# The down projection's left operands, made by the up projection's steps

## The chip, the cores and the metric

The kernel runs on one core of one Trainium2 chip. The number that counts is the device time of one execution in microseconds (us), as the median of several runs. The five engines are called as in the profile: PE (TensorE, the matmuls; PEld is its weight load), DVE (VectorE), ACT (ScalarE), POOL (GpSimd) and SP (SyncE, which here issues nearly all DMAs, in order).

## The reference: what is computed

One decoder block for 2048 tokens of width 1024, in float32. A norm and a combined input projection feed two token mixers that run side by side (a state space model with a GLU, and a delta-rule recurrence), whose outputs go through one output projection and are added to the input. The change touches only what comes after that, the MLP and the last norm:

```python
hn = rms_norm(h, norm_ffn_g[i])
h = h + jnp.square(jax.nn.relu(hn @ w_up[i].astype(F32))) @ w_down[i].astype(F32)
return rms_norm(h, norm_final_g).astype(x.dtype)
```

`w_up` is 1024 x 4096 and `w_down` 4096 x 1024, so the hidden layer is 2048 tokens x 4096.

## The kernel before

**Float32 out of three matmuls.** Every operand x is split into two numbers with few significant bits: hi is ACT's cast of x (L374, or L1418 in the up projection), lo is x - hi, computed on DVE (L377, L1419). A product of two operands is hi*hi + hi*lo + lo*hi, three matmuls per 128 rows of the inner dimension, all accumulated in one PSUM bank (`product`, L1328).

**Seven products instead of eight.** Both MLP projections use Winograd's form of Strassen's scheme once. Each operand is cut into four quarters a, b, c, d; seven products of sums of quarters give the four quarters of the result. `left_sums` makes the seven left operands, in the order 1, 5, 6, 2, 7, 3, 4 (`ORDER`): a; c + d; (c + d) - a; b; a - c; b - ((c + d) - a); d. Three of them (1, 2 and 4) are plain quarters and four (5, 6, 7 and 3) are sums, one tensor operation each (L1291, L1294, L1297, L1300). `right_sums` does the like for the right operand, again four operations (L1309, L1311, L1315, L1318). One PSUM bank A takes products 1, 6, 7 and 4 after each other and is read after each; bank X takes 5 and then 3; bank B takes 2.

**Up projection (`mlp_up`).** Its left operand is `w_up`, its right operand the normed rows of h. There are two halves of 1024 tokens (`hb`) and in each 16 steps (`f`) of 256 hidden columns, so 32 steps of seven products of twelve 512-wide matmuls. For each step 1 MB of weights is loaded (L1408) into the ring of eight buffers called `raw`, the left sums are made on POOL, and the halves go to a ring of 16 tiles, `ys`, from which PE loads them; they are made two products ahead (`UA`, class `Ahead`). What comes out of the seven products are four tiles of 128 hidden columns by 512 tokens: ACT copies a bank to SBUF (L1469), DVE adds another bank to it (L1495, L1498, L1501), and `finish` squares the relu: ACT relu (L1463), POOL square (L1464), then a store of 256 KB to DRAM, `hid_d` (L1465), on SP's queue. In the very last step three of the four tiles have relu and square in one DVE operation (L1461) and all four stores are on POOL's queue. When the first half of the tokens ends, the right operands of the second half are made (`xs`, L1397 and L1398, their sums on POOL).

**Down projection (`mlp_down`).** Its left operand is the hidden layer, its right operand `w_down`. Eight groups of 512 hidden rows each take all eight chunks of 256 tokens; a chunk of a group is seven products of six 512-wide matmuls. The 16 sums tiles `acc` (1024 wide, h at first) stay in SBUF. In a group's first chunk the seven right operands are taken; they are made from 2 MB of raw weights by DVE and ACT, in nine slots `w0` to `w8`, two products ahead (`DW`). The left operands are made anew for every chunk and group: two loads of 256 KB from `hid_d` (L1538, four buffers `hraw`), four sums 256 wide on POOL, seven casts on ACT and seven low halves on DVE, three products ahead (`DH`). Of a chunk's seven additions to `acc`, three go over an ACT copy (L1564) and POOL (L1560, from tile `c`), and four are DVE's, straight from PSUM (L1560). In the last group each chunk's rows are normed (ACT square into `junk`, L1594; DVE, L1596) and stored.

**Order.** The kernel is written in a framework that schedules the instructions of each engine by priority (the order of the program) against a model of time, gives tiles their buffers, and sets the waits. Each engine and each DMA queue then works in order. The first right and left operands of the down projection have high priority.

Of the kernel before, what the change touches and what calls it, by code (L numbers as in the profile page):

```python
# [15 lines left out]
P = 128  # L16
# [14 lines left out]
def exp_exact(nc, pool, out, x, n, tag):  # L31
    """out = exp(x), rounded to about one unit in the last place; 0 below the normal range."""
# [26 lines left out]
def sincos(nc, pool, s_out, c_out, x, n, tag):  # L59
# [42 lines left out]
    # even quadrant keeps (s, c), odd swaps them  # L102
# [11 lines left out]
def s5_params(K, lam_re, lam_im, log_dt, b_re, b_im, c_re, c_im, d_skip):  # L114
    """Everything of the state space that depends on the parameters alone.
    Rows of the 128 partitions: (re | im half, state 64); G = 32 groups of H = 16 channels; chunks of 16 tokens."""
# [4 lines left out]
    with pool_of(tc, name="s5p", bufs=1) as sp:  # L121
# [21 lines left out]
        # powers 0 .. 16 of exp(lam dt)  # L143
# [17 lines left out]
        # f = (exp(lam dt) - 1) / lam  # L161
# [17 lines left out]
        # b_bar, both halves  # L179
# [13 lines left out]
        # c, states on partitions, both halves  # L193
# [10 lines left out]
        # coefficient rows: c * power -> (re, -im), b * power -> (re, im)  # L204
# [13 lines left out]
        # chunk step exp(lam dt 16): [128 = (group half, state), re/im, 16 groups]  # L218
# [8 lines left out]
        # powers 1 .. 16 of the chunk step: real part, and -/+ imaginary part  # L227
# [21 lines left out]
def s5_core(K, u_dram, g_dram):  # L249
    """u_dram, g_dram: [2048, 512] token rows; g = gelu(state space of u + d_skip u)."""  # L250
# [17 lines left out]
    def out_rows(g):  # L268
        """two groups' c * power, [128, 2, 17 powers x 16 channels]"""
# [7 lines left out]
    for g in range(0, G, 2):  # L277
# [4 lines left out]
        # two groups' channels, newest token of a chunk first  # L282
# [30 lines left out]
    # running state over the 128 chunks, rows (group half, state), re and im side by side: within 8 segments of 16 chunks ...  # L313
# [11 lines left out]
    # ... then from segment to segment  # L325
# [55 lines left out]
def rms_rows(K, pool, ss, n, width, tag):  # L381
    """(ss / width + eps) ** -0.5 of [128, n] sums of squares."""
# [7 lines left out]
def norm_transposed(K, pool, ps_tile, rows, gain, dest, done=None):  # L390
    """rows: 4 tiles [128 tokens, 1024]; dest(k): where hi, lo go of rows * rms * gain, features 128 k .. on partitions."""
# [19 lines left out]
def norm_transposed_1(K, pool, ps_tile, row, gain, dest):  # L411
    """the same of one tile of 128 tokens, into dest[k]"""
# [16 lines left out]
def mm3(K, out, pairs):  # L429
    """out = sum over pairs of (lhs hi + lo)^T (rhs hi + lo) without the lo lo products (below float32's last bit)."""  # L430
# [1251 lines left out]
```

## Time and profile before

| | |
|---|---|
| median of three runs | 2687.09 us (2685.21 to 2688.03) |
| profiled execution, first to last instruction | 2688.6 us, taken as its own time |
| up projection, first to last matmul | 1272.6 to 1931.6 us |
| down projection, first matmul to the add of its last sum | 1938.3 to 2680.0 us |
| busy over the whole span | PE 92%, DVE 71%, POOL 52%, ACT 47% |
| mean granted TensorE clock | 0.968 |

A row of the table of stretches has the length and then the busy time of each engine with its number of instructions, the granted clock, the busy share of the DMA engines and the GB/s. A row of a group has line, engine, operation, output and inputs, shape, count, then busy time in us and mean ns of one, then the idle time just before them and what ended it. Rows of the chain of waits and of the timeline begin with the start and the length in us.

### The profile page before, as it was taken

How to read it: one execution, taken by the hardware profiler on the slowest of the kernel's cores; microseconds unless marked ns; L12 is line 12 of the kernel's file. 1: busy time of each engine (PE TensorE's matmuls, PEld its weight loads, DVE VectorE, ACT ScalarE, POOL GpSimd, SP SyncE). 2: the span in 40 equal slices, each digit the busy share in tenths (PEclk: the TensorE clock that was granted, in tenths of full speed). 3: DMA queues.
4: the chain of work that ended last, by engine and by line, in shares of the span. 5: the costliest groups of instructions: out<-in, count | busy, mean ns of one | idle time of the engine just before them, and what ended most of it. 6: DMA issues, size and time to landing. Idle time of an engine off the chain costs nothing. (4 is left out here: it accounts for less than half of the span.)

```text
span 2688.6 us, 38819 instructions
## 1 busy us (share of the span) xinstructions
PE 2476.8 (92%) x13084; PEld 2030.6 (76%) x13084; DVE 1906.8 (71%) x3212; ACT 1276.2 (47%) x2683; POOL 1387.2 (52%) x1261
## 2 busy tenths in 40 slices
PE   7999989998998989999999998999888899899987
PEld 7887667786888878887788877888666667677765
DVE  7468796679777868666844577444478878887877
ACT  6355545554444455454544444444334444444444
POOL 1068787503222233121655577555466666677666
PEclk9999989998989999999999999999899999999999
DMA  9555748896867453444453325232532212221213
GB/s 296 191 172 171 215 121 259 246 240 169 174 156 158 112 181 133 156 138 156 149 171 108 110 79 170 96 110 79 199 116 77 75 54 76 75 76 52 77 63 125
DMA packets 451799, 375.11 MB, mean 140 GB/s; under 512 B 182192, under 2 KB 382896, under 8 KB 451600
## 3 DMA queue, kind: packets, MB, share of 16 engines
q1 hardware_dynamic: 450992, 370.54, 46.1%
q8 instruction: 103, 1.69, 0.3%
q10 hardware_dynamic: 288, 1.05, 0.1%
q0 software_dynamic: 320, 1.05, 0.1%
q14 instruction: 96, 0.79, 0.1%
HBM read 245.55 MB, written 121.77 MB: 137 GB/s over the span
## 5 line engine op out<-in xcount | busy, mean ns | idle before, releaser
L1560 POOL TENSOR_TENSOR acc<-acc,c 128x512 f32<-128x512 f32 x192 | 282.2, 1488 | 43.2 <-ACT c L1564 42.9
L1464 POOL TENSOR_TENSOR c<-c 128x512 f32<-128x512 f32 x125 | 159.6, 1277 | 147.4 <-ACT c L1463 138.6
L377 DVE TENSOR_TENSOR hl<-hraw,hh 128x256 fp32r<-128x256 f32 x256 | 196.3, 785 | 28.8 <-ACT hh L374 28.2
L433 PE MATMUL ps_z<-xh,wh 128*128 128x512 f32 x448 | 184.6, 412 | 16.6 <-DVE zr L617 7.0
L1419 DVE TENSOR_TENSOR wl<-wraw,wh 128x512 fp32r<-128x512 f32 x128 | 154.1, 1217 | 52.6 <-ACT wh L1418 52.6
L374 ACT CAST hh<-hraw 128x256 fp32r<-128x256 f32 x256 | 103.3, 407 | 165.9 <-PE ps_da L1328 102.9
L435 PE MATMUL ps_z<-xh,wl 128*128 128x512 f32 x448 | 181.9, 406 | 0.0
L434 PE MATMUL ps_z<-xl,wh 128*128 128x512 f32 x448 | 181.3, 405 | 0.0
L374 ACT CAST hh<-hs 128x256 fp32r<-128x256 f32 x192 | 77.6, 406 | 190.3 <-PE ps_da L1328 90.3
L1419 DVE TENSOR_TENSOR wl<-ws,wh 128x512 fp32r<-128x512 f32 x96 | 92.4, 966 | 97.1 <-PE ps_ua L1328 57.5
L1560 DVE TENSOR_TENSOR acc<-acc,ps_dx 128x512 f32<-128x512 f32 x128 | 87.0, 680 | 95.4 <-POOL acc L1560 95.0
L1291 POOL TENSOR_TENSOR hs<-hraw 128x256 f32<-128x256 f32 x64 | 51.9, 810 | 167.8 <-DMA hraw<-hid_d 97.4
L913 POOL TENSOR_TENSOR DT<-dtc,cst 128x128 f32<-128x128 f32 x128 | 56.1, 469 | 158.9 <-PE ps_pq L920 106.1
L1418 ACT CAST wh<-ws 128x512 fp32r<-128x512 f32 x96 | 59.5, 620 | 145.3 <-PE ps_ua L1328 92.7
L377 DVE TENSOR_TENSOR hl<-hs,hh 128x256 fp32r<-128x256 f32 x192 | 122.8, 641 | 1.4 <-ACT hh L374 1.4
L433 PEld LDWEIGHTS ps_z<-xh,wh 128*128 128x128 f32 x448 | 87.6, 196 | 41.3 <-DVE zr L617 8.8
L1418 ACT CAST wh<-wraw 128x512 fp32r<-128x512 f32 x128 | 79.1, 619 | 80.7 <-PE ps_ua L1328 39.3
L1564 ACT COPY c<-ps_da 128x512 f32<-128x512 f32 x192 | 105.6, 583 | 14.4 <-PE ps_da L1328 14.4
L609 DVE TENSOR_TENSOR wl<-wr,wh 128x1024 fp32r<-128x1024 f32 x56 | 86.3, 1541 | 34.9 <-ACT wh L608 33.7
L433 PE MATMUL ps_o<-woh,ys 128*128 128x512 f32 x256 | 102.5, 401 | 1.5 <-ACT ys L1114 1.0
L435 PEld LDWEIGHTS ps_z<-xh,wl 128*128 128x128 f32 x448 | 87.3, 195 | 19.3 <-issue 0.5
L434 PEld LDWEIGHTS ps_z<-xl,wh 128*128 128x128 f32 x448 | 87.5, 195 | 18.7 <-issue 1.1
(673 smaller groups left out, 8434.5 us busy)
## 6 DMA issues: line engine op xcount, KB each, us to landing
wraw<-in_w_up SPq DMA_DIRECT2D x64, 512.0 KB
hraw<-hid_d SPq DMA_DIRECT2D x128, 256.0 KB
hid_d<-c SPq DMA_DIRECT2D x124, 256.0 KB
wr<-in_w_in SPq DMA_DIRECT2D x56, 512.0 KB
xrow<-in_x SPq DMA_DIRECT2D x32, 512.0 KB
wraw<-in_w_down SPq DMA_DIRECT2D x16, 1024.0 KB
aq<-f_d SPq DMA_DIRECT2D x32, 256.0 KB
ba<-f_d SPq DMA_DIRECT2D x64, 128.0 KB
```

The costliest lines, as they stand in the source:

```text
L374: nc.scalar.copy(out=hi, in_=raw)
L377: (lo_eng or nc.vector).tensor_tensor(out=lo, in0=raw, in1=hi.bitcast(F32), op=ALU.subtract)
L433: K.nc.tensor.matmul(out, lh, rh, start=i == 0, stop=False)
L434: K.nc.tensor.matmul(out, lh, rl, start=False, stop=False)
L435: K.nc.tensor.matmul(out, ll, rh, start=False, stop=i == n - 1)
L609: v.tensor_tensor(out=wl, in0=wr, in1=wh.bitcast(F32), op=ALU.subtract)
L913: g.tensor_tensor(out=DT[:, p], in0=bc(dtc[:, u, p:p + 1, :], [P, 4, 32]), in1=c["m4"].rearrange("p (a x) -> p a x", a=4), op=ALU.mult)
L1418: act.copy(out=hi, in_=o)
L1419: v.tensor_tensor(out=lo, in0=o, in1=hi.bitcast(F32), op=ALU.subtract)
L1464: g.tensor_tensor(out=o, in0=o, in1=o, op=ALU.mult)
L1560: add = lambda eng, o, s: eng.tensor_tensor(out=o, in0=o, in1=s, op=ALU.add)
L1564: act.copy(out=t, in_=ps)
```

## The change

The tiles that leave a step of the up projection are already the quarters that the down projection's `left_sums` needs, if its quarters are cut suitably: two neighbouring tiles of 128 hidden columns, and two blocks of 512 tokens. So the step itself makes the four sums (on DVE), their high halves (ACT) and low halves (DVE), and stores these eight tiles in `hs_d`; the three plain quarters are stored as they are, in `hr_d`. That makes eleven stores of 256 KB where there were four, all on SP's queue. The square goes from POOL to ACT, in every step; the last step has no special case any more, and product 4 is read by the relu without a copy before it.

The down projection loads, for two chunks at a time, the four ready operands (512 KB each, five buffers) and the three plain quarters (256 KB each, three buffers), and splits only the plain ones, 512 wide. Its rows of w and its token rows are paired anew to fit (`a i p`, `rows`). Of the three additions that POOL made, one (c2) goes to DVE. Tile counts change to make room: `raw` 8 to 7, `c` 5 to 3, and the last norm's `junk` shares the buffers of the loaded operands. The `ys` ring of 16 now also takes the hidden layer's halves.

```diff
-        raw = lambda shape, name: rp.tile(shape, F32, tag="raw", bufs=8, name=name)
+        raw = lambda shape, name: rp.tile(shape, F32, tag="raw", bufs=7, name=name)
...
+        def hid(name):
+            nonlocal ct
+            ct = (ct + 1) % 6
+            return hp.tile([P, BT], F32, tag="o", bufs=3, name=name) if ct < 3 else oc[0].tile([P, BT], F32, tag=("g2h", "g2l", "g2s")[ct - 3], name=name)
+
+        def operands(hb, fp, q, done):
+
+            def plain(n):
+                nc.sync.dma_start(out=hr_dram[hb, fp, PLAIN.index(n)], in_=q[n])
+
+            def split_(n, o):
+                hi, lo = (oy.tile([P, BT], F32R, tag="ys", bufs=16, name="h" + s) for s in "hl")
+                act.copy(out=hi, in_=o)
+                v.tensor_tensor(out=lo, in0=o, in1=hi.bitcast(F32), op=ALU.subtract)
+                for i, t in enumerate((hi, lo)):
+                    nc.sync.dma_start(out=hs_dram[hb, SPLIT.index(n), fp, i], in_=t.bitcast(F32))
+
+            if done in (1, 4):
+                plain(done)
+            elif done == 3:
+                a, c, d = q[1], q[3], q[4]
+                s = hp.tile([P, BT], F32, tag="s", bufs=2, name="hs")
+                v.tensor_tensor(out=s, in0=c, in1=d, op=ALU.add)
+                split_(5, s)
+                v.tensor_tensor(out=c, in0=a, in1=c, op=ALU.subtract)
+                split_(7, c)
+                q["s2"] = s2 = hp.tile([P, BT], F32, tag="s", bufs=2, name="hs2")
+                v.tensor_tensor(out=s2, in0=s, in1=a, op=ALU.subtract)
+                split_(6, s2)
+            else:
+                plain(2)
+                s = hp.tile([P, BT], F32, tag="s", bufs=2, name="hs3")
+                v.tensor_tensor(out=s, in0=q[2], in1=q["s2"], op=ALU.subtract)
+                split_(3, s)
...
-                def finish(o, fi, tb):
-                    if f == 30 and hb and (fi, tb) != (1, 0):
-                        v.scalar_tensor_tensor(out=o, in0=o, scalar=0.0, in1=o, op0=ALU.max, op1=ALU.mult)
-                    else:
-                        act.activation(out=o, in_=o, func=AF.Relu)
-                        g.tensor_tensor(out=o, in0=o, in1=o, op=ALU.mult)
-                    (nc.gpsimd if f == 30 and hb else nc.sync).dma_start(out=hid_dram[f + fi, :, (hb * 2 + tb) * BT:(hb * 2 + tb + 1) * BT], in_=o)
+                q = {}
+
+                def finish(o, name, src=None):
+                    act.activation(out=o, in_=o if src is None else src, func=AF.Relu)
+                    act.activation(out=o, in_=o, func=AF.Square)
+                    q[name] = o
+                    operands(hb, f // 2, q, name)
...
-                        c4 = t("c4")
-                        act.copy(out=c4, in_=A)
-                        finish(c4, 1, 0)
+                        finish(hid("c4"), 2, A)
...
         def hs():
...
+            for gr in range(NG):
+                for c in range(0, NC, 2):
+                    hb, tk, fs, ops = c // 4, slice(c % 4 * P, c % 4 * P + 256), slice(2 * gr, 2 * gr + 2), {}
+                    for i in range(2):
+                        for n in ORDER:
+                            if i:
+                                pass
+                            elif n in SPLIT:
+                                t = hp.tile([P, 2, 2, 256], F32R, tag="hs", bufs=5, name="hs")
+                                nc.sync.dma_start(out=t.bitcast(F32), in_=hs_dram[hb, SPLIT.index(n), fs, :, :, tk].rearrange("a l p t -> p a l t"))
+                                ops[n] = t[:, :, 0], t[:, :, 1]
+                            else:
+                                t = hp.tile([P, 2, 256], F32, tag="hr", bufs=3, name="hr")
+                                nc.sync.dma_start(out=t, in_=hr_dram[hb, fs, PLAIN.index(n), :, tk].rearrange("a p t -> p a t"))
+                                ops[n] = split(K, hp, t, [P, 2, 256], "h", 4)
+                            yield tuple([t[:, k, i * P:i * P + P] for k in range(2)] for t in ops[n])
...
-                    t = hp.tile([P, 512], F32, tag="c", bufs=5, name=name)
+                    t = hp.tile([P, 512], F32, tag="c", bufs=3, name=name)
                     act.copy(out=t, in_=ps)
-                    add(g, o, t)
+                    add(eng, o, t)
...
-                        later(a12, A, "c2")
+                        later(v, a12, A, "c2")
...
-                        junk = wp2.tile([P, 1024], F32, tag="junk", name="junk")
+                        junk = hp.tile([P, 1024], F32, tag="hs", bufs=5, name="junk")
```

The full diff also takes out comments all over the file, which changes line numbers little and no instruction.

More of the change, by code (lines that the diff above doesn't have):

```diff
@@ L1521, in mlp_down @@
         wpool, apool = [wp1] * 6 + [wp2] + [wp3] * 2, [rp] * 2 + [ap1] * 8 + [ap2] * 2 + [wp3] * 4
+        rows = lambda c: [(c // 4) * 1024 + i * BT + c % 4 * P for i in range(2)]
         def ws():
@@ L1533, in hs @@
         def hs():
-            for k in range(0, 32, 4):
-                for c in range(NC):
-                    r = [rp.tile([P, 2, 256], F32, tag="hraw", bufs=4, name="hraw") for _ in range(2)]
-                    for j in range(2):
-                        nc.sync.dma_start(out=r[j], in_=hid_dram[k + 2 * j:k + 2 * j + 2, :, c * 256:c * 256 + 256].rearrange("a p t -> p a t"))
-                    for o in left_sums(g, [[r[j][:, :, i * P:i * P + P] for j in range(2)] for i in range(2)],
-                                       lambda: hp.tile([P, 2, P], F32, tag="s", bufs=5, name="hs")):
-                        yield halves_of(K, hp, o, [P, 2, P], "h", 10)
+            for gr in range(NG):
[14 more added lines that the diff above has]
+                            yield tuple([t[:, k, i * P:i * P + P] for k in range(2)] for t in ops[n])
         w, hid = Ahead(ws(), DW), Ahead(hs(), DH)
-        acc, fin, first = [], None, None
+        acc, fin, first = {}, None, None
         with tc.high_priority():
@@ L1552, in mlp_down, with later @@
                   with tc.issue_after(first.ins) if c else ExitStack():
-                    for t in range(2 * c, 2 * c + 2):
-                        a = apool[t].tile([P, 1024], F32, tag=f"acc{t}", name=f"acc{t}")
-                        ld = nc.sync.dma_start(out=a, in_=h_dram[t * P:t * P + P, :])
-                        acc.append(a)
+                    for i in range(2):
+                        t = 2 * c + i
+                        acc[c, i] = apool[t].tile([P, 1024], F32, tag=f"acc{t}", name=f"acc{t}")
+                        ld = nc.sync.dma_start(out=acc[c, i], in_=h_dram[rows(c)[i]:rows(c)[i] + P, :])
                   first = first or ld
-                r0, r1 = acc[2 * c:2 * c + 2]
+                r0, r1 = acc[c, 0], acc[c, 1]
                 a11, a12, a21, a22 = r0[:, 0:512], r0[:, 512:], r1[:, 0:512], r1[:, 512:]
                 add = lambda eng, o, s: eng.tensor_tensor(out=o, in0=o, in1=s, op=ALU.add)
-                def later(o, ps, name):
-                    t = hp.tile([P, 512], F32, tag="c", bufs=5, name=name)
+                def later(eng, o, ps, name):
+                    t = hp.tile([P, 512], F32, tag="c", bufs=3, name=name)
                     act.copy(out=t, in_=ps)
-                    add(g, o, t)
+                    add(eng, o, t)
                 A, X, B = (psp.tile([P, BT], F32, tag=n, bufs=b, name="ps_d" + n) for n, b in (("a", 3), ("x", 2), ("b", 2)))
@@ L1596, in mlp_down @@
                         v.scalar_tensor_tensor(out=r, in0=r, scalar=rs, in1=fin, op0=ALU.mult, op1=ALU.mult)
-                        t0 = (2 * c + i) * P
-                        nc.sync.dma_start(out=out[0, t0:t0 + P, :], in_=r)
+                        nc.sync.dma_start(out=out[0, rows(c)[i]:rows(c)[i] + P, :], in_=r)
 _INS = ["x", "norm_mix_g", "w_in", "lam_re", "lam_im", "log_dt", "b_re", "b_im", "c_re", "c_im", "d_skip", "w_glu", "b_glu",
@@ L1627, in hybrid_block @@
         y_d = D([NT, 512], "y_d")
[L1628 removed]
+        x2_d, hs_d, hr_d = D([4, P, KT, BT], "x2_d"), D([2, 4, 16, 2, P, BT], "hs_d"), D([2, 16, 3, P, BT], "hr_d")
         A = lambda *names: [a[n] for n in names]
@@ L1661, in hybrid_block @@
             opened = out_proj(K, keep, a["x"], g_d, y_d, f_d, s_d, *A("g2", "ln_x_w", "ln_x_b", "w_glu", "b_glu", "s5_out_g", "w_out", "norm_ffn_g"), h_d, x2_d)
-            mlp_up(K, opened, h_d, x2_d, a["norm_ffn_g"], a["w_up"], hid_d)
-        mlp_down(K, h_d, hid_d, a["w_down"], a["norm_final_g"], out)
+            mlp_up(K, opened, h_d, x2_d, a["norm_ffn_g"], a["w_up"], hs_d, hr_d)
+        mlp_down(K, h_d, hs_d, hr_d, a["w_down"], a["norm_final_g"], out)
 def kernel(**inputs):
```

31 lines of the change are left out of this document (15 added, 16 removed).

## The prediction

> **What bounds the kernel now.** I read the busy shares first, then stretches of time: the up projection from its first matmul to its last, its undisturbed part, the down projection from its first matmul to the add of its last sum, and what is left behind it.
>
> ```profile
> PE 2476.8 (92%) x13084; PEld 2030.6 (76%) x13084; DVE 1906.8 (71%) x3212; ACT 1276.2 (47%) x2683; POOL 1387.2 (52%) x1261
> core 0: us, PE busy (x) PEld busy (x) DVE busy (x) ACT busy (x) POOL busy (x), PEclk, DMA share, GB/s
> 1272.60:1931.60 659.00, 636.66 (x2721) 510.95 (x2719) 360.14 (x357) 298.10 (x520) 382.34 (x268) 0.98 0.36 119
> 1660.00:1900.00 240.00, 240.00 (x1037) 193.79 (x1036) 113.36 (x123) 105.38 (x188) 129.26 (x99) 1.00 0.29 97
> 1938.30:2680.00 741.70, 662.88 (x2688) 509.18 (x2688) 605.07 (x819) 332.18 (x721) 512.37 (x460) 0.97 0.25 83
> 2680.00:2688.60 8.60, 0.00 (x0) 0.00 (x0) 3.38 (x5) 1.15 (x2) 1.10 (x2) 0.67 0.46 183
> ```
>
> PE is full in the undisturbed up projection (240 of 240 us); in the down projection DVE is at 605 of 742 us. Both stages issue 2688 matmuls. Their pace when nothing disturbs them is in the chain of waits, where the same product of two successive chunks begins 9.76 us apart:
>
> ```profile
> 2378.16 2.78 PE ps_da L1328 x12
> 2387.91 2.79 PE ps_da L1328 x12
> ```
>
> So a chunk (42 matmuls) costs 9.76 us, an up step (84) 19.52, and the 64 chunks 624.6 us. The down projection loses 741.7 - 624.6 = 117 us; the up projection 659.0 - 624.6 = 34, which its first steps and the change of token half lose. Cut into chunks, the sixth group of the down projection reads (the three rows left out are like the last but one):
>
> ```profile
> 2403.01:2416.88 13.87, 11.59 (x44) 8.96 (x42) 13.87 (x16) 6.05 (x13) 9.16 (x7) 0.88 0.19 57
> 2416.88:2426.69 9.81, 9.81 (x44) 7.90 (x43) 8.62 (x10) 5.21 (x11) 8.93 (x7) 1.00 0.39 135
> 2426.69:2440.26 13.57, 11.60 (x43) 8.97 (x42) 9.38 (x17) 4.20 (x10) 7.10 (x8) 0.87 0.19 58
> 2440.26:2450.04 9.78, 9.78 (x43) 7.89 (x42) 6.76 (x12) 4.20 (x10) 7.40 (x7) 1.00 0.18 55
> ...
> 2479.38:2492.39 13.01, 10.56 (x43) 7.66 (x42) 13.01 (x16) 5.23 (x12) 10.19 (x8) 1.00 0.30 103
> ```
>
> Three chunks lose 4.1 + 3.8 + 3.25 = 11.2 us, the others almost nothing; in two of the three DVE never rests. Over eight groups that is about 89 of the 117 us; the other 28 are spread over other groups' chunks.
>
> **The change, part by part: the down projection.** Its DVE work by groups:
>
> ```profile
> L377 DVE TENSOR_TENSOR hl<-hraw,hh 128x256 fp32r<-128x256 f32 x256 | 196.3, 785 | 28.8 <-ACT hh L374 28.2
> L377 DVE TENSOR_TENSOR hl<-hs,hh 128x256 fp32r<-128x256 f32 x192 | 122.8, 641 | 1.4 <-ACT hh L374 1.4
> L1560 DVE TENSOR_TENSOR acc<-acc,ps_db 128x512 f32<-128x512 f32 x64 | 43.2, 674 | 1.1 <-POOL acc L1560 1.1
> L1315 DVE TENSOR_TENSOR wraw<-wraw 128x1024 f32<-128x1024 f32 x8 | 16.7, 2088 | 0.0
> L1311 DVE TENSOR_TENSOR wraw<-wraw 128x1024 f32<-128x1024 f32 x8 | 12.6, 1574 | 0.0
> L1318 DVE TENSOR_TENSOR wraw<-wraw 128x1024 f32<-128x1024 f32 x8 | 11.9, 1487 | 0.0
> L377 DVE TENSOR_TENSOR w5l<-wraw,w5h 128x1024 fp32r<-128x1024 f32 x6 | 10.0, 1666 | 0.0
> ```
>
> All 448 low halves go: 319.1 us, 39.9 per group. Added per group: 12 low halves of plain quarters (512 wide) and 8 adds into acc that leave POOL (the one called c2), each a 512-wide operation with two SBUF inputs; at the 0.9 us found below, 18.0 us. The weights' share stays: four sums (5.15 for the three quoted, about 1.5 for the fourth) and seven low halves of about 1.5, 17.2 us. Apart from the weights DVE had 605.07 / 8 - 17.2 = 58.4 us per group, 7.3 per chunk; after, 58.4 - 39.9 + 18.0 = 36.5, or 4.6.
>
> The three chunks of weight work asked DVE for 3 x 7.3 + 17.2 = 39.1 us in 29.3: 9.8 too many, and they lose 11.2. After: 3 x 4.6 + 17.2 = 31.0, 1.7 too many. As a 2 us sum ahead of an add also holds up its bank, I keep 3.3 us per group, 26 in all (ends: none, and 89). The 28 us elsewhere go, with DVE at 4.6 of 9.76. POOL loses all 256 sums and 64 of its 192 adds of 1.49 us; ACT half its casts' width.
>
> New waits: PE now waits for loads themselves. A pair of chunks needs 4 x 512 + 3 x 256 KB, 2.9 MB in 19.5 us, 148 GB/s, with the weights' 2 MB per group 175: twice the 83 GB/s at a share of 0.25, so about 0.5. With five buffers for four tiles, the second to fourth tile waits for the last use of its predecessor's, eight products (11 us) ahead of its own. I take nothing (price in the rivals). The norm's junk now takes these buffers in the last group: 4 us (0 to 10). The first operands are 1.5 MB instead of 1 MB, and more must come early: 5 us.
>
> Down projection after: 624.6 + 26 + 4 + 5 = 660, so 82 us less; the 8.6 us tail stays.
>
> **The up projection.** Its undisturbed groups (1660 to 1900 us, 12.3 steps), and the slowest like them, at the change of token half (1570 to 1645 us, last row):
>
> ```profile
> L1419 DVE TENSOR_TENSOR wl<-wraw,wh 128x512 fp32r<-128x512 f32 x49 | 58.7, 1213 | 17.6 <-ACT wh L1418 17.6
> L1419 DVE TENSOR_TENSOR wl<-ws,wh 128x512 fp32r<-128x512 f32 x38 | 33.8, 890 | 47.6 <-PE ps_ua L1328 32.8 <-ACT wh L1418 14.8
> L1495 DVE TENSOR_TENSOR c<-c,ps_ub 128x512 f32<-128x512 f32 x12 | 8.3, 688 | 15.0 <-PE ps_ub L1328 15.0
> L1464 POOL TENSOR_TENSOR c<-c 128x512 f32<-128x512 f32 x50 | 62.9, 1258 | 59.2 <-ACT c L1463 59.2
> L1463 ACT ACTIVATE c<-c 128x512 f32<-128x512 f32 x50 | 30.6, 631 | 5.4 <-DVE c L1495 4.0 <-DVE c L1498 0.7 <-DVE c L1501 0.7
> L1418 ACT CAST wh<-wraw 128x512 fp32r<-128x512 f32 x49 | 30.4, 621 | 36.8 <-PE ps_ub L1328 19.1 <-PE ps_ua L1328 17.8
> ...
> L1419 DVE TENSOR_TENSOR wl<-wraw,wh 128x512 fp32r<-128x512 f32 x12 | 18.2, 1520 | 0.9 <-ACT wh L1418 0.9
> ```
>
> Per step DVE gets four sums and four low halves, ACT four squares (0.63) and four casts (0.62) and loses one copy (about 0.6); POOL loses four squares of 1.26. ACT goes from 105.38 / 12.3 = 8.6 to 13.0 of 19.5 us. The price of a 512-wide DVE operation with two SBUF inputs is the uncertain one: alone about the 0.69 of the PSUM row, with POOL at 129.26 / 12.3 = 10.5 us a step (58.7 + 33.8) / 87 = 1.06, at worst 1.52. POOL falls to 5.5 us, so 0.69 + 0.37 x 5.5 / 10.5 = 0.89. DVE per step: 15 x 0.89 + 3 x 0.69 = 15.4 of 19.5 us (12.4 at 0.69; 20.2 at 1.21). Beside it, three 20 us stretches:
>
> ```profile
> 1290.00:1310.00 20.00, 19.66 (x78) 15.37 (x77) 20.00 (x21) 11.13 (x20) 11.85 (x8) 0.91 0.42 146
> 1310.00:1330.00 20.00, 20.00 (x94) 16.29 (x93) 14.94 (x15) 12.14 (x24) 13.52 (x10) 1.00 0.42 129
> 1610.00:1630.00 20.00, 9.13 (x29) 6.63 (x28) 19.52 (x14) 9.29 (x14) 15.61 (x9) 0.78 0.67 210
> ```
>
> At 14.94 of 20 PE lost nothing, so 15.4 of 19.5 should hide: 3 us for all undisturbed steps (0; at 1.21, 26 x 0.7 = 18). Where DVE is full, what is added shows. At the start about eight operations, 7.2 us, less 1.2 for the squares gone from POOL: 6 (0 to 12). At the change of half two steps' 16, 14.4, less about half the time of seven squares that blocked DVE, 6: 8 (-5 to 14).
>
> The Trainium skill ("SBUF — State Buffer", section "Who interferes with whom") says that a DVE instruction with two SBUF inputs and a GpSimd instruction that reads SBUF shut each other out for the whole instruction. By that DVE can lose no more than POOL's own 5.5 us a step, 12.4 + 5.5 = 17.9 of 19.5: undisturbed steps would cost 0 rather than the 18 us of the 1.21 row. The means agree in kind (0.69 alone, 1.52 where POOL is busiest); whether it holds at this DVE load no run here shows yet.
>
> Stores go from four to eleven of 256 KB a step. All are in SP's queue, where the next weight loads stand behind stores that wait for DVE's halves.
>
> ```profile
> 1709.71 0.38 SPq L1408 DMA_DIRECT2D wraw<-in_w_up  x1
> 1710.89 0.32 SPq L1465 DMA_DIRECT2D hid_d<-c  x1
> 1618.54 1.74 POOL L1291 TENSOR_TENSOR ws<-wraw 128x512 f32<-128x512 f32 x1 [3.95 <-DMA wraw<-in_w_up]
> 1931.18 0.39 PE L1328 MATMUL ps_ua<-x4h,wl 128*128 128x512 f32 x1
> 1938.26 0.79 PE L1328 MATMUL ps_da<-w0h,hh 128*128 128x512 f32 x1 [6.68 <-ACT hh L374]
> ```
>
> Issue: 11 x 0.32 + 2 x 0.38 = 4.3 us of SP a step; 3.9 MB per step, 201 GB/s, a share near 0.6 by the 0.29 at 97. A load is a step ahead, which hides the wait; at the change of half that cover is gone already (POOL waits 3.95 us for weights), which is in the 8 us. At the handover the last step's relu, square and casts, formerly in part DVE's and with stores on POOL's queue, stand on ACT before the cast that PE waits 6.68 us for: 5 us (0 to 10).
>
> Sum: -82 + 6 + 8 + 3 + 5 = -60. The profiled execution's own time is its span, 2688.6 us, 1.5 above the median of the runs, 2687.1. So 2628.6 by span, 2627 as median.
>
> **Rivals.** (A, slower) DVE becomes the bound of the up projection. From a mean of 1.16 us per two-SBUF operation a step passes 19.52; from about 1.30 (2.1 us in each of 28 steps) the 60 us are eaten; at 1.5, 24.6 us a step, it gives 2688.6 - 60 + 28 x 5.05 = 2770. For it: 1.52 at the change of half. Against: POOL's work halves. (B, about no change) The weight chunks keep their 89 us, since weight sums stand ahead of adds whatever else DVE does: gain 28, less 22, 2682 by span. For it: a losing chunk where DVE had only 9.38 of 13.57. Against: the work count above. (C) Operand loads come late by 1.2 us a pair: 32 x 1.2 = 38, 2667. For it: 2.9 times the bytes; against: a share near 0.5. (D) The change doesn't do what it says, DVE in the down projection staying near 605 us: nothing speaks for it, the removed instructions are counted.
>
> **Chances.** My forecast 0.60 (its own range, from the ends above, 2588 to 2660), C 0.12, B 0.14, A 0.13, D 0.01. A measurement of this kernel tells about 0.2%, 5 us, from no change. Faster: 0.60 + 0.12 + half of B, 0.79; same: 0.07; slower: A and 0.01, 0.14. Range for 8 in 10: 2585 to 2690.
>
> **What would show it.** Right: down chunks near 9.76 us with losses only in a few weight chunks; DVE there near 430 us; up steps at 19.5 with DVE near 79% and POOL near 28%; over 35 us at the change of half. Wrong: up steps over 20 us, PE in the down projection waiting for the stored operands' loads, or three chunks per group still near 13 us.

## The result, and the profile after

The change makes the kernel slower, by 0.9%. The median goes from 2686.16 us (2685.21 to 2688.03; a fourth run moved it a little from the 2687.09 above) to 2708.97 us (2704.92 to 2715.55), a ratio of 1.009 with a 95% interval of 1.0073 to 1.0106. The forecast was 2627 us.

The busy line of the page after, and rows of the table of stretches (columns as in the prediction) for the up projection, its undisturbed part, the down projection and the tail (span 2709.7 us, before 2688.6):

```profile
PE 2486.5 (92%) x13084; PEld 2027.1 (75%) x13084; DVE 1910.2 (70%) x3177; ACT 1307.2 (48%) x2558; POOL 926.5 (34%) x812
1266.50:2005.40 738.90, 667.30 (x2721) 507.58 (x2719) 544.55 (x603) 427.27 (x743) 234.98 (x141) 0.97 0.51 180
1700.00:1920.00 220.00, 210.29 (x871) 160.15 (x870) 156.66 (x184) 129.35 (x227) 60.95 (x40) 1.00 0.52 182
2029.20:2702.50 673.30, 642.96 (x2688) 509.84 (x2688) 423.39 (x530) 231.53 (x369) 201.97 (x143) 0.98 0.53 177
2702.50:2709.70 7.20, 0.00 (x0) 0.00 (x0) 2.65 (x4) 1.15 (x2) 0.55 (x1) 0.63 0.36 146
```

The down projection did get shorter, 741.7 to 673.3 us, but the up projection grew from 659.0 to 738.9 us and the gap between the two from 6.7 to 23.8. In the undisturbed stretch PE does 871 matmuls in 220 us where before it did 1037 in 240: 3.96 against 4.32 per us. So the step of 84 matmuls is 21.2 us, not 19.5. Yet DVE is busy for only 156.66 of 220 us there, ACT for 129 and POOL for 61, at full granted clock and half the DMA engines' time. No engine is full, and PE still loses.

The first four steps and the four steps around the change of token half (the 16th to the 19th), before and then after:

```profile
1272.60:1369.70 97.10, 86.91 (x369) 68.75 (x368) 68.29 (x65) 53.93 (x96) 61.60 (x39) 0.93 0.50 166
1584.00:1677.60 93.60, 81.86 (x338) 65.00 (x337) 75.66 (x55) 46.09 (x75) 75.18 (x43) 0.95 0.40 127
```

```profile
1266.50:1380.10 113.60, 90.68 (x369) 70.00 (x368) 82.89 (x84) 63.07 (x113) 43.67 (x24) 0.89 0.57 195
1614.20:1727.60 113.40, 88.07 (x337) 66.67 (x336) 94.46 (x87) 62.91 (x102) 49.16 (x24) 0.88 0.48 167
```

What is left of the up projection, its 24 other steps, is 659.0 - 97.1 - 93.6 = 468.3 us before and 738.9 - 113.6 - 113.4 = 511.9 after. The balance, with the forecast's terms:

| part | forecast, us | measured, us |
|---|---|---|
| 24 other up steps | +3 | +43.6 |
| first four steps | +6 | +16.5 |
| change of half | +8 | +19.8 |
| gap between the projections | +5 | +17.1 |
| down projection | -82 | -68.4 |
| tail | 0 | -1.4 |
| begin of the up projection, which the change doesn't touch | 0 | -6.1 |
| sum | -60 | +21.1 |

The last row but one is within the spread of runs: in the runs quoted below, whose code up to there is the same, the up projection begins between 1266.5 and 1276.4 us.

**Where a steady step loses its time.** The chain of waits after, one step of the undisturbed stretch and the beginning of the next two (start, length, what):

```profile
1786.09 8.35 PE ps_ua L1328 x36
...
1794.47 0.61 ACT c L1499
...
1795.76 1.65 DVE hs L1491
...
1798.62 0.73 PE ps_ua L1328 x2
...
1819.83 0.73 PE ps_ua L1328 x2
```

PE finishes product 4, ACT makes relu and (in the line left out) square of its tile, DVE the last of the four sums, ACT the high half of that sum, and only then the high half of a weight operand, for which PE waits. That weight has nothing to do with the sum: its cast only stands behind the sum's cast on ACT. The timelines of ACT, POOL and DVE show it:

```profile
1797.43 0.62 ACT L1471 CAST hh<-hs 128x512 fp32r<-128x512 f32 x1 [1.70 <-DVE hs L1491]
1797.95 0.61 ACT L1423 CAST wh<-ws 128x512 fp32r<-128x512 f32 x1
1795.55 1.30 POOL L1300 TENSOR_TENSOR ws<-wraw,ws 128x512 f32<-128x512 f32 x1 [11.62 <-DVE wl L1424]
1794.72 0.68 DVE L1424 TENSOR_TENSOR wl<-ws,wh 128x512 fp32r<-128x512 f32 x1
```

ACT sits idle for 1.70 us in front of the sum's cast, with the weight's cast behind it. From the end of product 4 to the next product 6 pass 4.2 us (1794.44 to 1798.62), in which PE has only product 5 to do, 2.8 us, since the scheduler has put the next product 1 ahead of product 4. The next time round it is 21.21 us later (1819.83). It is a closed loop: each step's matmuls wait for a result of the step before.

The chain names relu and square as what the sum waits for, but they are not what ends last. In all ten steps of the stretch the sum ends 2.96 us after product 4, whether it starts 1.33 us after it and takes 1.63 us, or 1.67 us after it and takes 1.29; the same kind of operation takes 0.69 us elsewhere in the step. It ends each time 0.55 us behind POOL's weight sum. That one starts when DVE has made product 5's low half (1794.72 + 0.68), which stands on DVE behind the step's other three sums and their low halves. So the loop runs over PE, DVE, POOL, DVE again and ACT.

### The profile page after: what moved, and what is told of

It is laid out like the page before. It is cut to its first block, busy times and chain, and to the rows that moved or that the text cites. A ratio compares the mean times of both kernels' runs of the same rounds, so it can differ in the third digit from the quotient of the medians.

```text
span 2709.7 us, 38217 instructions
## 1 busy us (share of the span) xinstructions
PE 2486.5 (92%) x13084; PEld 2027.1 (75%) x13084; DVE 1910.2 (70%) x3177; ACT 1307.2 (48%) x2558; POOL 926.5 (34%) x812
## 4 chain that ended last, share of the span: by engine, by line
PE 59%; DVE 16%; DMA 10%; issue 6%; ACT 5%; POOL 3%; SPq 1%; POOLq 0%; DVEq 0%; ACTq 0%
PE ps_ua L1328 12%; PE ps_da L1328 9%; PE ps_dx L1328 4%; PE ps_ux L1328 3%; PE ps_ub L1328 3%; PE ps_db L1328 2%; DMA wraw<-in_w_down 2%; PE ps_o L435 2%; PE ps_o L433 2%; PE ps_o L434 2%; DVE hs L1491 2%; PE ps_z L433 1%; PE ps_z L434 1%; PE ps_z L435 1%; PE ps_b L817 1%
## 5 line engine op out<-in xcount | busy, mean ns | idle before, releaser
L1605 POOL TENSOR_TENSOR acc<-acc,c 128x512 f32<-128x512 f32 x128 | 193.8, 1535 | 482.0 <-ACT c L1609 436.4
L1424 DVE TENSOR_TENSOR wl<-wraw,wh 128x512 fp32r<-128x512 f32 x128 | 163.2, 1301 | 4.6 <-ACT wh L1423 1.8
L1300 POOL TENSOR_TENSOR ws<-wraw,ws 128x512 f32<-128x512 f32 x32 | 43.5, 1360 | 347.7 <-DVE wl L1424 342.1
L1499 ACT ACTIVATE c<-c 128x512 f32<-128x512 f32 x96 | 60.6, 631 | 165.8 <-DVE c L1532 101.5
L374 ACT CAST hh<-hr 128x512 fp32r<-128x512 f32 x96 | 59.6, 621 | 125.6 <-PE ps_da L1328 88.6
L433 PE MATMUL ps_o<-woh,ys 128*128 128x512 f32 x256 | 102.6, 401 | 1.5 <-ACT ys L1114 0.9
L434 PE MATMUL ps_o<-wol,ys 128*128 128x512 f32 x256 | 101.6, 398 | 0.0
L435 PE MATMUL ps_o<-woh,ys 128*128 128x512 f32 x256 | 100.7, 397 | 0.0
L1471 ACT CAST hh<-hs 128x512 fp32r<-128x512 f32 x96 | 59.8, 623 | 58.2 <-DVE hs L1491 49.7
L377 DVE TENSOR_TENSOR hl<-hr,hh 128x512 fp32r<-128x512 f32 x96 | 67.9, 712 | 26.1 <-ACT hh L374 25.9
L1500 ACT ACTIVATE c<-c 128x512 f32<-128x512 f32 x128 | 81.0, 633 | 3.5
```

The lines of the kernel that those rows point to most:

```text
L377: (lo_eng or nc.vector).tensor_tensor(out=lo, in0=raw, in1=hi.bitcast(F32), op=ALU.subtract)
L433: K.nc.tensor.matmul(out, lh, rh, start=i == 0, stop=False)
L434: K.nc.tensor.matmul(out, lh, rl, start=False, stop=False)
L435: K.nc.tensor.matmul(out, ll, rh, start=False, stop=i == n - 1)
L1424: v.tensor_tensor(out=lo, in0=o, in1=hi.bitcast(F32), op=ALU.subtract)
L1471: act.copy(out=hi, in_=o)
```

## The experiments

Each ratio is to runs of the kernel before that were taken along with the run (medians between 2689.44 and 2695.43 us). Stretches and waits are those of one profiled execution each.

**Three weight operands ahead.** With `UA` at 2, the operand of a step's product 6 is asked for when the step's product 1 is issued, which in the program is just behind the last sum of the step before. With 3 it is asked for one product earlier, ahead of that sum. No instruction is added or removed.

```diff
-UA, DW, DH = 2, 2, 3
+UA, DW, DH = 3, 2, 3
```

> The changed kernel with the up projection's left operands made three products ahead instead of two. Theory of the loop: the cast of product 6's weights then stands ahead of the last sum's cast, the step falls to 19.5 to 20.0 us, the kernel by 30 to 48 us; a smaller gain if the 16 tiles that weights and hidden halves share run short, since one more pair is now alive. Rival, throughput: no change of the step, 21.2 us.

2661.53 us, ratio 0.9871 (0.9847 to 0.9895): 2.2% under the change, some 59 us, more than expected, as the start and the change of half gain too. Stretches of this run: the first four steps, the four around the change of half, and a stretch behind them:

```profile
1275.10:1382.10 107.00, 89.76 (x370) 69.58 (x369) 77.02 (x85) 63.23 (x114) 43.89 (x25) 0.90 0.62 209
1596.60:1705.90 109.30, 86.88 (x338) 66.79 (x337) 84.00 (x87) 62.40 (x102) 53.50 (x24) 0.88 0.51 173
1700.00:1900.00 200.00, 200.00 (x865) 161.47 (x864) 134.50 (x182) 128.13 (x225) 56.26 (x41) 1.00 0.57 199
```

PE is full, 200 of 200 us (865 matmuls, the pace of the kernel before), with all of the change's sums, splits and stores in place. DVE is busy for 67% of the time. So the work did fit under PE, and the loop was the whole loss of the undisturbed steps. The last sum still meets POOL in every step here (mean of ten 1.282 us), and PE loses nothing: the meeting costs time only where a weight's cast stands behind the sum's.

**The same depth in the kernel before.** The same one-number edit in the kernel before (`UA` 3).

> The kernel before with three weight operands ahead instead of two. Its undisturbed up steps are at the pace of the matmuls already, so by the loop theory the third operand is worth nothing there: 0.996 to 1.001. Rival (three ahead is a gain of its own, whatever the change does): under 0.99.

2689.3 us, ratio 0.9993 (0.9979 to 1.0006). Three ahead is worth nothing by itself; it is worth 2% only together with the change.

**The last sum later in the program.** With two ahead, the last sum and its split are issued behind product 6 of the next step.

```diff
-                    operands(hb, f // 2, q, name)
+                    if name == 2:
+                        late.append((hb, f // 2, q, name))
+                    else:
+                        operands(hb, f // 2, q, name)
...
                         c2 = copy(A, "c2")
+                        while late:
+                            operands(*late.pop())
```

> The changed kernel with one edit: the last sum of a step, its two halves and the two stores that go with it (what follows product 4) come in the program after product 6 of the next step instead of at once, so ACT's cast of that sum stands behind the weight casts of the next products. Theory of the loop: an undisturbed up step takes 21.2 us instead of 19.5 because product 4's end, ACT's relu and square, DVE's last sum, ACT's cast of it and, behind it in ACT's queue, the cast of the weights that product 6 of the next step needs form a closed chain of 4.2 us with only product 5 (2.8 us) to cover it. Then the step falls to 19.5 to 20.0 us and the whole kernel by 27 x 1.2 to 1.7, 32 to 48 us, to about 2665. Rival, throughput of DVE with POOL at the shared port: the work is the same, so the step stays at 21.2 and the time near 2709.

2709.76 us, ratio 1.005 (1.0031 to 1.0069): a gain of 0.4% on the change, not the one expected. In the chain of this run the first loop is gone, and a second one sets the pace of every other step (steps alternate between 20.3 and 21.2 us, a few are longer):

```profile
1792.37 0.70 DVE c L1541
...
1794.42 0.70 DVE hs L1481
...
1796.36 1.89 DVE hl L1472 x3
1798.24 0.62 DVE wl L1424
```

Here a weight's low half stands on DVE behind the three sums and splits that follow product 3's tile. Asking for weights earlier breaks every such loop; moving one piece of work breaks one.

**A second relu, on the chain or off it.** It takes 0.63 us on ACT and has no effect on the values. It is on the tile of product 4, which the chain of waits runs through (`name == 2`, as below), or on the tile of product 2, which it doesn't (`name == 1`):

```diff
+                    if name == 2:
+                        act.activation(out=o, in_=o, func=AF.Relu)
                     act.activation(out=o, in_=o, func=AF.Square)
```

> The changed kernel with a second relu on the tile that product 4 gives (the same values come out). Theory of the loop: the added 0.63 us of ACT, less 0.1 of overlap, lies on the chain, so the undisturbed step grows from 21.2 to 21.7 to 21.9. Rival, throughput of DVE: ACT has a third of its time to spare, so the step stays at 21.2.

> The changed kernel with the same second relu on the tile of product 2 instead, which does not lie on the chain. Theory of the loop: no change, 21.2 us a step. If ACT's or any engine's total were the bound, it would grow as in the kernel with the relu on product 4's tile.

One run each, 2737.89 and 2718.82 us; single runs of one kernel differ by 5 to 10 us here, so the steady stretch is the better witness. First with the relu on product 4's tile (and its last sum, from the chain), then on product 2's:

```profile
1700.00:1920.00 220.00, 207.88 (x856) 156.87 (x854) 151.72 (x184) 134.77 (x236) 61.31 (x41) 1.00 0.53 187
1810.88 0.98 DVE hs L1491
```

```profile
1700.00:1920.00 220.00, 210.28 (x870) 159.82 (x871) 160.73 (x187) 134.19 (x237) 65.81 (x43) 1.00 0.53 184
```

The same 0.63 us of ACT work cost PE 15 matmuls of 871 on the one tile (856) and one on the other (870). But on product 4's tile a step grew by only 0.3 us (mean 21.6 against 21.3), and the trace shows that the relu itself is absorbed. In two steps of three the sum starts 0.66 us later by it and takes 0.97 us instead of 1.63: it ends 2.96 us after product 4 as before, behind the same POOL operation, and product 6 follows after 4.2 us as before. In every third step product 6 follows after 4.8 us, since there the scheduler has put ACT's copy of product 5's bank ahead of the weight's cast. So this pair of runs shows that ACT's total is not the bound; that relu and square are part of the loop it does not show.

**The squares alone.** The kernel before with its squares on ACT and nothing else of the change.

```diff
-                        g.tensor_tensor(out=o, in0=o, in1=o, op=ALU.mult)
+                        act.activation(out=o, in_=o, func=AF.Square)
```

> The kernel before with one part of the change alone: the up projection's squares on ScalarE in place of GpSimd (the last step's special form stays as it was). Loop theory (the new step length comes from the chain that runs through the sums and their splits to the next step's weights): without the sums no chain returns to TensorE, so the undisturbed up steps stay at 19.48 us and the time is 0.998 to 1.002 of the kernel before. Rival (the squares' 4 x 0.64 us on ScalarE, which also makes the weights' high halves, lengthen the steps): steps of 20 to 21 us, 1.005 or more.

2691.18 us, ratio 1.0009 (0.9996 to 1.0022). The undisturbed steps stay full and the change of half gets 5 us shorter (88.5 us for the four steps), but something new shows at the gap. Stretches (first four steps, change of half, undisturbed, down projection), PE's waits (what it waited for: us in total, times, longest) and ACT's timeline:

```profile
1271.30:1367.90 96.60, 87.11 (x370) 68.96 (x369) 64.48 (x63) 59.48 (x108) 46.97 (x27) 0.93 0.51 166
1582.10:1670.60 88.50, 81.44 (x338) 64.66 (x337) 65.09 (x54) 54.63 (x89) 49.57 (x24) 0.94 0.41 131
1700.00:1900.00 200.00, 200.00 (x864) 161.48 (x863) 72.17 (x103) 112.77 (x195) 51.07 (x39) 1.00 0.28 93
1945.70:2675.90 730.20, 662.20 (x2688) 509.56 (x2688) 597.78 (x809) 329.24 (x717) 507.01 (x455) 0.98 0.23 76
PE ps_da L1328 <- ACT hh L374: 20.8, 1, 20.8
1940.74 1.04 ACT L374 CAST w2h<-wraw 128x1024 fp32r<-128x1024 f32 x1 [6.75 <-DVE wraw L1311]
1945.29 0.40 ACT L374 CAST hh<-hraw 128x256 fp32r<-128x256 f32 x1
```

In the kernel before PE waited 6.7 us at this place. Here the scheduler, with other work on ACT, has put the casts of all seven weights ahead of the first left operand's, two of them with long waits for DVE's sums, and PE waits 20.8 us. No added work explains 14 us: it is the order in which ACT got its casts. Much of it is won back, as the weights of the whole first group are ready when it begins (the down projection takes 730.2 us instead of 741.7).

**The gap between the projections.** After the change, PE waits for the first weight's high half. PE's wait, SP's timeline and ACT's:

```profile
PE ps_da L1328 <- ACT w0h L374: 23.6, 1, 23.6
2010.97 0.53 SPq L1467 DMA_DIRECT2D hr_d<-c  x1
2019.09 1.30 SPq L1565 DMA_DIRECT2D wraw<-in_w_down  x2
2022.65 1.37 ACT L374 CAST hh<-hr 128x512 fp32r<-128x512 f32 x2 [8.36 <-DMA hr<-hr_d]
2028.05 1.04 ACT L374 CAST w0h<-wraw 128x1024 fp32r<-128x1024 f32 x1 [4.03 <-DMA wraw<-in_w_down]
```

Two things hold it: the raw weights are asked for at 2019.09, 14 us behind the last product, since their loads stand on SP behind the last step's stores and the first operands' loads; and on ACT the casts of four plain operands, waiting for their own loads, stand ahead of it. In the chain of waits the last of these operand loads goes out only when the store issued at 2010.97 has landed, 6.82 us later, although it reads what the first half of the tokens stored (`hb` 0); which wait holds it there is not shown. All the following have three weights ahead. In the first, the first group's w_down loads go to POOL's queue:

```diff
-                    nc.sync.dma_start(out=r[i], in_=wk[i])
+                    (nc.gpsimd if k == 0 else nc.sync).dma_start(out=r[i], in_=wk[i])
```

> Three weight operands ahead, and the first group's four w_down loads issued by GpSimd instead of SyncE. If the gap of TensorE between the projections is SyncE's in-order queue (the loads stand behind the last step's stores and the loads of those stores), the gap goes from 26 us to 8 to 12 us and the time is 14 to 18 us under that with three ahead alone: 0.980 to 0.983 of the kernel before. Rival (the loads wait for the memory under them or for bandwidth, wherever they are issued): the gap stays over 20 us, 0.985 to 0.988.

2655.34 us, ratio 0.9871 (0.9854 to 0.9888): not distinguishable from three ahead alone, and a miss. PE waits 21.0 us, where it waits 25.7 with three ahead alone; the weights are there in time, but the casts aren't:

```profile
1972.22 1.37 ACT L374 CAST hh<-hr 128x512 fp32r<-128x512 f32 x2 [8.46 <-DMA hr<-hr_d]
1973.50 1.04 ACT L374 CAST w0h<-wraw 128x1024 fp32r<-128x1024 f32 x1
```

The next two also have the scratch tile's edit shown further below (0.9842 by itself). One issues the first chunk pair's seven operand loads and the weights' from POOL (`nc.sync if gr or c else nc.gpsimd` in `hs`), the other the last step's eleven stores (`nc.gpsimd if hb and fp == 15 else nc.sync` in `operands`):

> Three weight operands ahead, the norm's scratch tile in the raw weights' buffer, and all loads of the down projection's first chunk pair (the seven of left operands and the first four of w_down) issued by GpSimd, ahead of nothing of SyncE's. With the weights alone moved, the gap fell only from 26 to 21 us, because ScalarE took the splits of the plain operands first and waited there for loads that still stood behind SyncE's stores. If that queue is the whole cause, the gap now falls to 8 to 13 us: 0.977 to 0.980 of the kernel before, against 0.984 without it. Rival (the loads wait for the stores' data to land, or for bandwidth, whichever queue issues them): the gap stays at 19 us or more, 0.982 to 0.985.

> The other way around: the loads stay with SyncE and the last step's eleven stores are issued by GpSimd (the kernel before issued its last step's stores so). By the queue theory the gap falls from 25 us to 8 to 15 us: 0.977 to 0.981 of the kernel before. By the rival (data or bandwidth) it stays at 19 us or more, 0.982 to 0.985.

2651.39 us, 0.9842 (0.9824 to 0.9861), and 2648.4 us, 0.9836 (0.9819 to 0.9853); PE waits 27.5 and 19.4 us, where it waits 25.1 without them. Both miss: a change of queue alone gives at most 6 us, and with all the first loads on POOL's queue the wait is longer.

Then the casts. The first group's first plain operands are split on POOL, and the first weights are loaded from ACT's queue, or from POOL's:

```diff
-                                ops[n] = split(K, hp, t, [P, 2, 256], "h", 4)
+                                ops[n] = split(K, hp, t, [P, 2, 256], "h", 4, *((g, g) if gr == 0 and c < 4 else ()))
```

> Three weight operands ahead, the scratch tile in the raw weights' buffer, the splits of the first group's first plain left operands on GpSimd (idle there), and the first group's w_down loads issued by ScalarE right behind its last cast of the up projection. If the handover's loss is the in-order work of ScalarE (the first weight's high half stands behind splits that wait for late operand loads), the loads go out at the end of the last product plus 5 us, land 8 us later, and the gap is 12 to 16 us against 25: 0.979 to 0.981 of the kernel before (0.984 without). Rival (the operand loads are late in themselves): the gap stays over 19 us, 0.982 to 0.985.

> The same with the first w_down loads issued by GpSimd, where their place is behind the first two plain operands' splits. If GpSimd's order now holds the weights back as ScalarE's did, the gap is 17 to 22 us, longer than with the loads on ScalarE; if lateness of loads in general is the cause, the two are alike within 2 us.

2651.03 us, 0.9853 (0.9836 to 0.9871), and 2650.94 us, 0.985 (0.983 to 0.987). PE's first wait is 23.8 and 21.4 us. Both miss. The timelines of ACT in the one and of POOL in the other:

```profile
1967.70 3.64 ACTq L1565 DMA_DIRECT2D wraw<-in_w_down  x2
```

```profile
1965.91 1.64 POOL L1565 DMA_DIRECT2D wraw<-in_w_down  x2
```

ACT had nothing to do from 1957.5, but its loads went out only at 1967.70, just after an `hr_d` store of SP's, 6.85 us under way, had landed; POOL's stood behind its own splits. So both got the weights late again, by another way. The last kernel avoids both: weights loaded by POOL, early, and only the third and later plain operands split on POOL (`c == 2 or c == 0 and n == 4` in place of `c < 4`).

> Three weight operands ahead, the scratch tile in the raw weights' buffer, the first w_down loads issued by GpSimd (they landed before the last product ended when this was done alone), and GpSimd also makes the splits of the third and fourth plain left operands, so that only two stand ahead of the first weight's on ScalarE. Those two operands land some 5 and 10 us after the last product. If order and load are the whole handover loss, the first weight's high half is made some 11 us after the last product and the gap falls from 25 us to 11 to 14 us: 0.979 to 0.981 of the kernel before. If something else keeps TensorE, the gap stays over 18 us and the time at 0.982 to 0.985.

2643.63 us, ratio 0.9819 (0.9796 to 0.9841), the lowest of all, though its interval overlaps that of the scratch tile alone. PE's waits, and two lines of the chain of waits:

```profile
PE ps_da L1328 <- ACT w0h L374: 11.1, 1, 11.1
PE ps_da L1328 <- POOL hh L376: 7.5, 1, 7.5
1960.86 6.46 DMA hs_d<-hh
...
1968.14 6.80 DMA hr<-hr_d
```

The weight comes when expected, after 11.1 us, but two matmuls later PE waits 7.5 us more for a plain operand whose load came late. The two waits are 18.6 us, not the 11 to 14 expected, so order and load of the weight are not the whole loss: of 25 us they are 6; what remains is the late operand loads. In the chain of this run, the last two lines above, such a load begins behind a store on SP that takes 6.5 us to land and takes 6.8 itself. That these two are the rest is read from the chain, not shown by a run that removes them.

**The last group of the down projection.** It takes 94.3 us with three ahead where the floor is 78. Its scratch tile for the norm goes into a buffer of the raw weights, which are done by then; or the output's stores go to POOL's queue:

```diff
-                        junk = hp.tile([P, 1024], F32, tag="hs", bufs=5, name="junk")
+                        junk = rp.tile([P, 2, 1024], F32, tag="wraw", bufs=2, name="junk")[:, 0]
```

> Three weight operands ahead, and the norm's scratch tile in a buffer of the raw weights (done by then) instead of one of the operands' five. By the queue theory the last group stays within 3 us of 94.3 us; by the scratch-tile theory, which is the one of the prediction, it falls to 83 to 86 us.

> Three weight operands ahead, and the output's stores issued by GpSimd instead of SyncE. If the last group of the down projection is lengthened by operand loads that stand behind output stores which SyncE holds back until the rows are normed, the last group goes from 94.3 us to 83 to 86 us: 0.983 to 0.985 of the kernel before. Rival (the norm's scratch tile, which shares its buffers with the operands): the last group stays within 2 us of 94.3, 0.986 to 0.988.

2647.08 us, 0.9842 (0.9819 to 0.9865), and 2652.38 us, 0.9866 (0.9848 to 0.9884). The last group with three ahead, then with the scratch tile moved, then with the stores moved:

```profile
2562.70:2657.00 94.30, 83.92 (x338) 65.70 (x336) 56.37 (x83) 38.03 (x67) 30.21 (x31) 0.95 0.49 167
```

```profile
2553.50:2635.00 81.50, 78.94 (x337) 62.59 (x336) 56.59 (x83) 37.84 (x67) 30.37 (x31) 1.00 0.55 188
```

```profile
2552.30:2638.70 86.40, 79.52 (x338) 62.46 (x336) 58.28 (x83) 37.70 (x67) 38.84 (x44) 1.00 0.52 177
```

The theory that stood behind these two runs, SP's queue alone, fell: the scratch tile is worth 12.8 us, the whole loss but 3.4. But moving the stores alone wins 7.9 us, so the rival that they matter nothing fell too. The queue makes the scratch tile's loss worse: the chain of the changed kernel has an operand load right behind an output store that waited for the norm:

```profile
2661.04 0.33 SPq L1642
...
2661.42 4.40 DMA hs<-hs_d
```

A load whose buffer the scratch tile has taken is issued late, and then stands behind that store.

**The start and the change of half.** With three ahead, they still lose 10 and 16 us more than before. In one kernel the sums of the step ahead of the change of half are left out (a hidden tile is stored in their place, so that step's share of the output is wrong); in the other the kernel before has squares on ACT and seven `raw` buffers in place of eight.

> Three weight operands ahead; in the one step ahead of the half change the sums and their splits are left out (a hidden tile is stored in their place, so the output is not the reference's). The half change (four steps from the 16th) takes 109 us with the sums and 88 us in the kernel before with the squares alone moved. If the sums' eight VectorE and four ScalarE instructions, which run beside GpSimd's sums of the right operands, make the difference, it falls to 90 to 97 us; if it is the loads of the right operands behind SyncE's stores, it stays over 104 us.

> The kernel before with the squares on ScalarE and seven raw buffers in place of eight; no sums, no other change. If the missing buffer is what remains of the half change and the start, the step ahead of the half change (the 16th) grows from 19.48 to 22 us or more, the first four steps from 96.6 us to over 100, and the time is 1.003 to 1.006; if not, all stay within 1 us and the time is 0.999 to 1.002.

2656.37 us, 0.9867 (0.9845 to 0.9889), and 2696.5 us, 1.0017 (1.0004 to 1.003). The change of half without the sums; then, with seven buffers, the first four steps and the change of half:

```profile
1594.00:1693.30 99.30, 85.55 (x337) 66.52 (x336) 80.75 (x79) 59.80 (x98) 51.81 (x24) 0.93 0.55 191
```

```profile
1273.40:1375.20 101.80, 86.42 (x369) 68.54 (x369) 65.56 (x65) 61.13 (x109) 45.96 (x27) 0.90 0.48 159
1589.50:1677.10 87.60, 80.51 (x338) 64.49 (x337) 66.18 (x54) 54.49 (x89) 47.26 (x24) 0.96 0.40 132
```

The one step's sums cost 10 us (109.3 to 99.3), less than the 12 to 19 expected. The missing buffer costs the start 5 us (96.6 with eight and the squares on ACT) and the change of half nothing; in the medians, 1.0017 against 1.0009 with eight, it can't be told. What the other 11 us of the change of half are (99.3 against 88.5) stays open, as do some 5 us of the start.

## Why the prediction was wrong

- **The undisturbed up steps: the step that failed.** "At 14.94 of 20 PE lost nothing, so 15.4 of 19.5 should hide." The amount was right: DVE has 156.66 of 220 us, 15.1 a step against 15.4, and ACT 12.5 against 13.0. The inference was wrong. A busy share says whether the work fits, not whether it is done in time, and the comparison stretch held no sum between PE's last product and a weight. The prediction did price the sums as work and did not ask the other question: what stands behind each waiting instruction on ACT and DVE? The last sum waits until POOL's weight sum is done, ACT's cast of it waits for the sum, and the next weight's cast is behind that one. That made 43.6 us in place of 3. With three ahead the step's own words hold: 19.5 us, nothing lost.
- **Rival A** gave the right sign, and it named DVE beside POOL, but as a bound on DVE's time. For that it needed a mean of 1.16 us per two-SBUF operation; the mean was 0.89 and DVE stayed at 71%. What POOL did was to hold back one sum that a weight's cast stood behind. The steps over 20 us, named as the sign that would refute the forecast, came all the same.
- **The price of a DVE operation** beside POOL, 0.89 us by estimate, was right: 156.66 us less the 21.9 of the 32 operations that read PSUM, over 152 operations, is 0.89. Three of the group rows of DVE after, 1700 to 1920 us:

```profile
L1424 DVE TENSOR_TENSOR wl<-wraw,wh 128x512 fp32r<-128x512 f32 x40 | 51.1, 1306 | 1.8 <-ACT wh L1423 0.9
L1472 DVE TENSOR_TENSOR hl<-hs,hh 128x512 fp32r<-128x512 f32 x30 | 20.6, 688 | 6.9 <-ACT hh L1471 6.9
L1491 DVE TENSOR_TENSOR hs<-c,hs 128x512 f32<-128x512 f32 x10 | 15.0, 1495 | 4.9 <-ACT c L1500 4.9
```

  The same kind of operation takes 0.69 us where POOL rests and 1.3 to 1.5 where it works. The last sum of a step, the one in the loop, meets POOL's `ws` every time (1.29 to 1.64 us, mean of ten 1.495). In the step shown it takes 1.65 us and ends at 1797.41, half a microsecond behind POOL's operation (1795.55 + 1.30). The Trainium skill ("SBUF — State Buffer", section "Who interferes with whom") has the two shut each other out for a whole instruction; these rows agree. The sentence drawn from it, that undisturbed steps would cost 0, was a bound on the amount of work and says nothing of a loop in which that wait falls. Here the meeting takes 0.6 to 0.9 us of the 1.7 that a step loses (1.29 or 1.63 against 0.69 us), as an estimate, for no run removes it alone.
- **The start and the change of half** (6 and 8, measured 16.5 and 19.8): the mechanism, work added where DVE is full, is part of it (10 us of the change of half, by the run without the sums); the loop takes 6.6 of the start (113.6 to 107.0) and 4.1 of the change of half (113.4 to 109.3), the lost `raw` buffer, which the prediction did not price at all, 5 of the start.
- **The handover** (5, measured 17.1): mis-sized, and for want of a question. The prediction counted instructions added ahead of the cast that PE waits for. What the runs showed in its place: the squares alone, which change the order of ACT's casts, made the wait 20.8 us, against 6.7 before. Order and late weights were 6 of the 25 us with three ahead; the late operand loads, which stand among the last step's stores on SP, are the rest as the chain has it, and the cause of their wait stays open.
- **The down projection** (-82, measured -68.4): the mechanism was right. DVE is at 423.39 us where about 430 was forecast, and undisturbed chunks run at PE's pace. The mis-sized term is the last group's scratch tile, 4 us forecast and 12.8 measured; without it the projection takes 660.5 us (673.3 - 12.8), where 656 were forecast for the rest. The other groups lose about 5 us each against eight chunks of 9.76, where 3.3 were kept for the weights.
- **Rivals B, C and D** did not occur: the first seven groups together lose some 34 us, against 98 before (counted from the starts of every 42nd matmul), and in the down projection loads are late only at its begin and in its last group, where PE waits for them three times, 7.2 us in all. B's sum was wrong besides: it leaves out the 4 and 5 us that the forecast itself adds to the down projection, so it should have been 2691 by span, not 2682. And the forecast's own range, 2588 to 2660, does not follow from the ends named for its terms, which add up to 57 us below and 101 above 2627.

With the loop, the scratch tile and part of the handover mended, the change brings 50 of the 60 us forecast: 2643.63 us against 2694.01.

## What to carry to other kernels

Before adding work "under" a full engine, write down what each engine has queued behind the new waiting instruction, and follow it until it reaches the full engine again; if the path closes within one iteration, its length is the new period, however idle everyone is. The cure here was to ask for the other operands one product earlier in program order, and the test is one number. In the chain of waits, look also at what lengthens an operation while it runs: a chain shows what an operation started after, not that another engine held it from then on. At the handover between the stages, a scheduler's order of casts and a queue's order of loads and stores mattered more than the sum of their work, so look at these orders again after each edit, also one that touches nothing there.

## What the runs showed of the hardware

- A loop over PE, DVE, POOL and ACT, with DVE at 71%, ACT at 59% and POOL at 28%, held a step at 21.2 us where its matmuls need 19.5.
- A 512-wide DVE operation with two SBUF inputs took 0.69 us alone and 1.63 us when it met a POOL operation; started 0.66 us later it took 0.97 and ended at the same time, 0.55 us behind POOL's operation, so that this delay was won back whole.
- A 256 KB store at the handover took 6.5 to 6.9 us to land, and loads issued by ACT, which was idle, also did not go out before; which wait held them was not tested.
